# Activation forms moved to other steps, and one split of 1536 columns for the three plain weight units, in a feed-forward loop on one Trainium2 core

## The chip, the cores and the metric

The kernel runs on one core of a Trainium2 chip. The metric is the device time of one execution in microseconds, as the median of several runs. The engines are named as the profile names them: PE is TensorE (PEld its weight loads), DVE VectorE, ACT ScalarE, POOL GpSimd, and SP is SyncE, which here only issues DMAs. Every engine works through its own queue in order and waits at an instruction until what it needs from the others is there.

## The reference

A block of an encoder on 256 tokens of width 2048: two gated branches, an output projection, a layer norm, and a feed-forward part with a second layer norm. Only the feed-forward part matters here:

```python
mix = merged @ w_out[l]
h = _layernorm(DEEPNORM_ALPHA * h + mix, ln1_g[l], ln1_b[l])
ff = jnp.square(jax.nn.relu(h @ w_ff1[l])) @ w_ff2[l]
h = _layernorm(DEEPNORM_ALPHA * h + ff, ln2_g[l], ln2_b[l])
```

w_ff1 is 2048 x 8192 and w_ff2 is 8192 x 2048, both float32.

## The kernel before

Every float32 operand of a matmul is used as a sum of two parts, a high one (hi) and the remainder (lo). ScalarE makes hi by a cast (`cast`, line 1103), VectorE makes lo by a subtraction (`rest`, line 1106). A product is then three matmuls: hi by hi, hi by lo and lo by hi. Weights come from memory as blocks of 1 MB (128 x 2048), and are split on their way.

The hidden width of 8192 is worked on as four quarters of 16 channel blocks. The first product of a quarter (h by w_ff1, `channel_products`, line 141) is made channel block by channel block: eight matmuls of 512 columns and eight of 256 for each half of a block. The second product (by w_ff2) uses, for the first three quarters, a scheme with seven products of sums and differences of activation blocks and weight blocks in place of eight (`FORM`, line 1071, and `join_sums`, line 1262); the last quarter is multiplied directly (`Quarter`, `token_products`).

`ff_pairs` (line 1278) has 48 steps s, and 16 of them are called a phase. In each step it makes one channel block of the next quarter and the seven products of one pair of row blocks of the present one. In the order of the program a step is:

1. three products with the plain weight units (`form_products` which=0, 9 matmuls). Then `plain_split(s + 1)` (line 1156): casts and subtractions of three units of 512 columns, two sums within the raw tile on VectorE, and two DMAs on POOL's queue that add within the raw tile;
2. two products with the first two sums (6 matmuls), and the first half of the channel block;
3. `half_split(s + 1, 0)` and `pair_split(s + 1)`, then two products of the step before (6 matmuls) and `last_split(s)`. These splits are one cast and one subtraction of 1024 columns each;
4. SP's load of the raw tile for step s + 2, and the second half of the channel block;
5. `quad_sum` (line 1109): the channel block's two parts are added out of PSUM, a copy on ScalarE (tile f_l) and a sum on VectorE (tile fr); then `half_split(s + 1, 1)` with SP's load of another block;
6. at some steps `forms` (line 1123), and at odd s `squares` (line 1117), two activations of 512 columns on ScalarE.

Two channel blocks fill one quad tile of 128 x 4 x 128 (`quads`, a ring of five tiles). `forms` turns a finished quad into the seven activation forms of a slot: four casts on ScalarE and six small operations on VectorE, which depend on each other in turn. In the last quarter (`plain`) a form is one cast and one subtraction. There are eight slots (`fa_slot`). Step s reads slot s mod 8, and which=2 reads it once more in step s + 1, so that in a phase of 16 steps slot i is read last in steps 8 + i and 9 + i, and is needed with its new content in step 16 + i. Before, slot i is filled at the end of step 9 + i (line 1305):

```python
if s >= 9 and (s - 9) % 16 < 8:
    forms((s - 9) % 16, s >= 2 * 16 + 9)
```

The last one falls behind the loop and is made in `ff_close` (line 1321).

After each group of eight steps the seven sums are taken out of PSUM (`take_sum`, line 1251), in steps 7, 15, 23 and so on: in the first phase by VectorE (three, with a scale) and ScalarE (four), later by VectorE alone (seven of 512 columns).

The channel products of a step have one PSUM buffer: three of the pool's four are held by sums (w2, w3 and w4), so the next channel block starts when `quad_sum` has read the last one. The tiles of the plain units, `xh` and `wx`, have one buffer each: the cast for step s + 1 waits until the plain products of step s have been made.

Most casts, sums and high-part matmuls of the loop are kept in program order by `pin` (line 1097). What is not pinned, the channel products among it, is ordered by the scheduler when the kernel is built. `ep` is a pool with one buffer for each tag; `turn0` and `turn1` (line 969) are two small tiles of the first layer norm that share a tag and so follow each other. `block_load` (line 1194) puts the blocks of w_ff1 into the tags `xl` and `fraw`.

Of the kernel before, what the change touches and what calls it, by code (L numbers as in the profile page):

```python
# [9 lines left out]
F32 = mybir.dt.float32  # L10
F32R = mybir.dt.float32r
# [5 lines left out]
P = 128  # L17
D = 2048
# [25 lines left out]
def block_kernel(  # L44
# [28 lines left out]
    base = ctx.enter_context(tc.tile_pool(name="base", bufs=1))  # L73
# [175 lines left out]
    with tc.tile_pool(name="xp", bufs=1) as xp, tc.tile_pool(name="xq", bufs=1) as xq:  # L249
        def units(pool, tag, n, **kw):  # L250
            t = pool.tile([P, n, OPENING * P], F32R, tag=tag, name=f"open_{tag}", **kw)
            return lambda a, b: t[:, a:b].rearrange("p k (b j) -> p k b j", b=OPENING)

        pieces = {}
        for k0, n in PIECES[::-1]:
            if k0 < 10:
                pieces[k0] = xp.tile([P, n, KROW], F32, tag=f"xw{k0}", name=f"xw{k0}")
            else:
                raw = wp.tile([P, D], F32, tag="raw", bufs=3, name=f"xw{k0}")
# [15 lines left out]
        for i in range(3):  # L275
            t = weight_half(-1, i)
# [17 lines left out]
        for k0, n in PIECES:  # L294
            raw = pieces[k0]
# [12 lines left out]
            if k0 == 0:  # L308
                hi, lo = places[0]
# [165 lines left out]
    for i in range(2 * NCH):  # L475
        c, o = divmod(i, 2)
        n = 4 + (i * 21) // 15
# [421 lines left out]
    ep = ctx.enter_context(tc.tile_pool(name="ep", bufs=1))  # L899
# [66 lines left out]
    rows1 = load_rows(0)  # L966
    turn_b, turn_i = dfth, dftl
    for i, t in ((0, turn_b), (1, turn_i)):
        raw = ep.tile([P, 1024], F32, tag="wx", name=f"turn{i}")[:, 0:512].rearrange("p (a b) -> p a b", b=P)
        nc.scalar.dma_start(raw, ln_turn[i])  # L970
        nc.scalar.copy(t, raw)
        if i == 0:
            nc.vector.tensor_tensor(t[32:64], raw[32:64], t[32:64].bitcast(F32), op=ALU.subtract)
# [11 lines left out]
    x0 = tuple(ep.tile([P, D], F32R, tag=t, name=t) for t in ("xh", "xl"))  # L985
# [43 lines left out]

    def begin_three():  # L1030
        blocks = [queue.popleft(), [], []]
        hx, lx = (ep.tile([P, D], F32R, tag=t, name=f"{t}_f") for t in ("xh", "xl"))
        at = 0
        for b in (1, 2):
            n = fetched[0]
            fetched[0] = n + 1
            raw = wp.tile([P, D], F32, tag="raw", bufs=3, name=f"raw{n}")
            nc.sync.dma_start(raw, wblk[n])
            for h in range(2):
                src = raw[:, h * 1024:(h + 1) * 1024]  # L1040
                if b + h == 2:
                    hi, lo = hx[:, at:at + 1024], lx[:, at:at + 1024]
                    at += 1024
                    with tc.issue_after(scaled[0].ins):
                        nc.scalar.copy(hi, src)
                    with tc.issue_after(turned[1][1].ins):
                        nc.vector.tensor_tensor(lo, src, hi.bitcast(F32), op=ALU.subtract)
                elif b == 1:
                    hi, lo = weight_half(n, h)
                    split_hi_lo(hi, lo, src)  # L1050
                else:
                    hi, lo = n, src
                blocks[b].append((hi, lo))
        begun = [(channel_psum(f"f0_{b // 2}_{b % 2}"), parts, 1 if b == 2 else 2) for b, parts in enumerate(blocks)]
        for at, size in CHUNKS:
            for ps, parts, n in begun:
# [32 lines left out]
    quad_tiles = [base.tile([P, 4, P], F32, tag=t, name=f"fr{i}") for i, t in enumerate(("dfth", "dftl", "sum"))]  # L1089
    quad_tiles += [ep.tile([P, 4, P], F32, tag=f"fr{i}", name=f"fr{i}") for i in (3, 4)]  # L1090

    def quads(i):
        return quad_tiles[i % 5]

    pinned = [False]

# [6 lines left out]
    def cast(hi, src):  # L1103
        return pin(nc.scalar.copy(hi, src))  # L1104
# [12 lines left out]
    def squares(i):  # L1117
        q = quads(i)
        pin(nc.scalar.activation(q, q, AF.Relu))
        return pin(nc.scalar.activation(q, q, AF.Square))  # L1120


    def forms(i, plain=False):
        q, slot = quads(i), fa_slot(i)
        hi, lo = slot[:, 0], slot[:, 1]
        if plain:
            cast(hi[:, 0:4], q)
            rest(lo[:, 0:4], q, hi[:, 0:4])
            return
        t = base.tile([P, 2, P], F32, tag="as", name=f"fw{i}")  # L1130
        cast(hi[:, 0:3], q[:, 1:4])
        VT(t, q[:, 0:1].broadcast_to([P, 2, P]), q[:, 1:3][:, ::-1], ALU.subtract)
        cast(hi[:, 3:5], t)
        VT(q[:, 0], q[:, 1], t[:, 0], ALU.subtract)
        rest(lo[:, 0:3], q[:, 1:4], hi[:, 0:3])
        VT(q[:, 2], q[:, 3], q[:, 0], ALU.subtract)
        cast(hi[:, 5:7], q[:, 0:3:2])
        rest(lo[:, 3:5], t, hi[:, 3:5])
        rest(lo[:, 5:7], q[:, 0:3:2], hi[:, 5:7])
# [4 lines left out]
            return fa_slot(kt // 2)[:, part, ((1, 0), (3, 2))[kt % 2][ts.start // P]]  # L1144

    SLOTS = 48

    def ring_load(p):
        nc.sync.dma_start(ring_tile(p), wblk[FF_PAIRS + 2 * p])
# [5 lines left out]

    def plain_split(p):
        raw, n = ring_tile(p), FF_PAIRS + 2 * p
        hi = ep.tile([P, D], F32R, tag="xh", name=f"b_h{p}")
        lo = ep.tile([P, 1024], F32R, tag="wx", name=f"b_l{p}")
        u = units(raw)  # L1160
        at = slice(0, 1024), slice(1024, 1536)
        low = lo, hi[:, 1536:2048]
        for c in at:
            cast(hi[:, c], raw[:, c])
        for c, dst in zip(at, low):
            rest(dst, raw[:, c], hi[:, c])
# [111 lines left out]
    def ff_pairs():  # L1278
        pss = [psum_side(f"w{j}") if j not in (2, 3, 4) else psum_main(f"w{j}") for j in range(7)]
        joins = []  # L1280
        for s in range(SLOTS):
            more = s + 1 < SLOTS
            pinned[0] = True
            form_products(pss, s, 0, (0, 1, 2))
            if more:
                plain_split(s + 1)
            form_products(pss, s, 1, (3, 4))
            ps = channel_psum(f"f{s // 16 + 1}_{s % 16}")
            channel_products(ps, hT, half_parts.pop((s, 0)), range(8))
# [11 lines left out]
            i, c = divmod(s % 16, 2)  # L1301
            quad_sum(i, c, ps, f"f{s // 16 + 1}_l{s % 16}")
            if more:
                half_split(s + 1, 1)
            if s >= 9 and (s - 9) % 16 < 8:
                forms((s - 9) % 16, s >= 2 * 16 + 9)
            if c:
                squares(i)
            if joins:
                joins.pop(0)()  # L1310
            pinned[0] = False
            if s == SLOTS - 2:
                stop_at[0] = nblk - 4
                fetched[0] = FF_PAIRS + 2 * SLOTS
            for _ in range(max(0, s - SLOTS + 3)):
                fetch()
        return pss, joins

    def ff_close(pss, joins):
        form_products(pss, SLOTS - 1, 2, (5, 6))  # L1320
        forms(7, True)
        for j in joins + join_sums(1):
            j()

# [25 lines left out]
    def quarters(*tiles):  # L1350
# [4 lines left out]
    own = [ep.tile([P, n], F32R, tag=t, name=f"{t}_r")  # L1355
           for t, n in (("xh", D), ("xl", D), ("fraw", D))]
# [201 lines left out]
```

## Time and profile before

| | before |
|---|---|
| runs, us | 1818.03, 1818.08, 1817.70; median 1818.03 |
| the profiled execution, us | 1818.21, with a span of 1816.4 |
| busy in the span, us | PE 1797.7, PEld 1505.1, DVE 1454.9, ACT 1042.5, POOL 164.8 |
| mean granted clock of TensorE | 0.999 |
| ff_pairs | first weight load of step 0 at 1199.11 us, of step 47 at 1706.84 us |

The page gives busy time by engine. The waits give who waited for whom, with the total, the count and the longest. The table by stage gives busy time in chosen stretches, and the timeline the instructions in order of time: start, duration, engine, line, operation, output and inputs, and in brackets the idle time ahead of it and who ended it. Where instructions of one kind follow each other they are merged, with their count at the end. Matmul records overlap: one of 512 columns shows 0.39 us, and the next begins 0.23 us after it.

### The profile page before, as it was taken

The numbers are of one execution on the slowest core, as the hardware profiler recorded it, in microseconds if no ns is written. First come the engines' busy times: TensorE is split into PE (matmuls) and PEld (weight loads), VectorE is DVE, ScalarE is ACT, GpSimd is POOL, SyncE is SP. The second block draws the span as 40 slices with busy tenths as digits, with TensorE's granted clock in tenths as the row PEclk, the third lists the DMA queues.
The fourth block names the chain that finished last, engine by engine and source line by source line (L and its number), as shares of the span: only waits on it lengthen the run. The fifth ranks groups of instructions, "written<-read, shape, count | busy, mean of one in ns | idle before, by whom it ended". The sixth has DMA issues, their size and how long they took to land.

```text
span 1816.4 us, 23481 instructions
## 1 busy us (share of the span) xinstructions
PE 1797.7 (99%) x8787; PEld 1505.1 (83%) x8787; DVE 1454.9 (80%) x1893; ACT 1042.5 (57%) x1423; POOL 164.8 (9%) x217
## 2 busy tenths in 40 slices
PE   9999999999999999999999999999999999999998
PEld 7888888888888888888888889888877887788887
DVE  6789887875689899988755667688889888989867
ACT  6678668865344444444544445666666566666632
POOL 1011110000111101010000000011111111111100
PEclk9999999999999999999999999999999999999999
DMA  8678876445798979797555764578777977789663
GB/s 324 227 256 292 249 230 200 149 163 204 229 297 250 308 248 283 251 278 258 197 187 186 310 235 159 187 213 248 236 227 235 275 235 221 221 255 273 214 219 127
DMA packets 79283, 424.77 MB, mean 234 GB/s; under 512 B 9817, under 2 KB 12393, under 8 KB 38465
## 3 DMA queue, kind: packets, MB, share of 16 engines
q1 hardware_dynamic: 47808, 336.61, 50.5%
q0 software_dynamic: 24304, 66.99, 18.2%
q10 hardware_dynamic: 7056, 19.67, 3.1%
q8 instruction: 69, 1.13, 0.3%
q14 instruction: 46, 0.37, 0.1%
HBM read 381.86 MB, written 16.25 MB: 219 GB/s over the span
## 4 chain that ended last, share of the span: by engine, by line
PE 87%; DVE 7%; ACT 3%; issue 3%; DMA 1%; ACTq 0%; DVEq 0%; POOL 0%
PE f L147 9%; PE f L151 5%; PE g L200 3%; PE g L199 3%; PE g L201 3%; PE ux L199 3%; PE ux L200 3%; PE ux L201 3%; PE w L1245 3%; PE w L1244 3%; PE w L1246 3%; PE k L147 2%; PE v L201 2%; PE v L200 2%; PE v L199 2%
## 5 line engine op out<-in xcount | busy, mean ns | idle before, releaser
L86 ACT CAST whi<-raw 128x1024 fp32r<-128x1024 f32 x392 | 412.7, 1055 | 408.6 <-PE ux L201 84.4
L87 DVE TENSOR_TENSOR wlo<-raw,whi 128x1024 fp32r<-128x1024 f32 x392 | 477.1, 1221 | 206.8 <-ACT whi L86 205.5
L147 PE MATMUL f<-hT,whi 128*128 128x512 f32 x984 | 246.4, 395 | 2.4 <-DVE fr L1101 1.9
L147 PEld LDWEIGHTS f<-hT,whi 128*128 128x128 f32 x984 | 180.4, 189 | 44.4 <-DVE fr L1101 10.1
L151 PEld LDWEIGHTS f<-hT,wlo 128*128 128x128 f32 x984 | 132.3, 190 | 8.7
L151 PE MATMUL f<-hT,wlo 128*128 128x256 f32 x984 | 135.0, 282 | 0.0
L1101 DVE TENSOR_TENSOR wlo<-fraw,whi 128x1024 fp32r<-128x1024 f32 x96 | 117.0, 1219 | 11.8 <-ACT whi L1104 11.8
L1169 POOL DMA_DIRECT2D ring<-wblk x48 | 41.7, 869 | 723.0 <-DVE ring L1101 723.0
L1104 ACT CAST whi<-ring 128x1024 fp32r<-128x1024 f32 x48 | 50.6, 1054 | 90.6 <-DVE ring L1101 83.8
L1104 ACT CAST whi<-fraw 128x1024 fp32r<-128x1024 f32 x96 | 100.7, 1049 | 0.2 <-PE f L147 0.2
L200 PE MATMUL g<-wlo,xT 128*128 128x512 f32 x256 | 100.1, 391 | 0.0
L201 PE MATMUL ux<-whi,xT 128*128 128x512 f32 x256 | 99.9, 390 | 0.0
L201 PE MATMUL g<-whi,xT 128*128 128x512 f32 x256 | 99.8, 390 | 0.0
L200 PE MATMUL ux<-wlo,xT 128*128 128x512 f32 x256 | 99.6, 389 | 0.0
L199 PE MATMUL g<-whi,xT 128*128 128x512 f32 x256 | 93.8, 392 | 0.0
L199 PE MATMUL ux<-whi,xT 128*128 128x512 f32 x256 | 89.7, 389 | 0.0
L1101 DVE TENSOR_TENSOR b_l<-ring,b_h 128x1024 fp32r<-128x1024 f32 x48 | 58.7, 1224 | 33.1 <-ACT b_h L1104 33.0
L1104 ACT CAST b_h<-ring 128x1024 fp32r<-128x1024 f32 x96 | 74.9, 829 | 8.8 <-ACT whi L1104 8.2
L1101 DVE TENSOR_TENSOR ring<-ring 128x512 f32<-128x512 f32 x96 | 66.0, 688 | 1.6
L1101 DVE TENSOR_TENSOR wlo<-ring,whi 128x1024 fp32r<-128x1024 f32 x48 | 58.8, 1225 | 2.7 <-ACT whi L1104 1.2
L1101 DVE TENSOR_TENSOR fa<-ring,fa 128x1024 fp32r<-128x1024 f32 x48 | 58.5, 1219 | 0.8 <-ACT fa L1104 0.8
L1104 ACT COPY f_l<-f 128x256 f32<-128x256 f32 x64 | 23.7, 370 | 61.1 <-PE f L147 58.2
(538 smaller groups left out, 4345.4 us busy)
## 6 DMA issues: line engine op xcount, KB each, us to landing
raw<-wblk SPq DMA_DIRECT2D x204, 1024.0 KB, 5.1
fraw<-wblk SPq DMA_DIRECT2D x48, 1024.0 KB, 7.1
ring<-wblk SPq DMA_DIRECT2D x48, 1024.0 KB, 6.2
Td<-T POOLq DMA_DIRECT2D x32, 384.0 KB, 5.4
conv_sb<-conv_rows SPq DMA_DIRECT2D x12, 1024.0 KB, 11.5
Tl<-Td POOLq DMA_DIRECT2D x16, 768.0 KB, 9.4
ring<-wblk POOLq DMA_DIRECT2D x48, 256.0 KB, 4.3
ring<-ring POOLq DMA_DIRECT2D x48, 256.0 KB, 5.0
```

Of the source, the lines that this page charges most:

```text
L86: return (nc.scalar.copy(hi, src), nc.vector.tensor_tensor(lo, src, hi.bitcast(F32), op=ALU.subtract))
L87: nc.vector.tensor_tensor(lo, src, hi.bitcast(F32), op=ALU.subtract))
L147: MM(ps[:, :, ts], hi[:, js], act[:, kt, :, ts], start=(kt == 0 and opens), stop=(kt == KT - 1))
L151: MM(ps[:, 0, ts], lo[:, js], act[:, kt, 0, ts], start=False, stop=False)
L199: MM(pss[tb], sh, wh, start=(kt == 0), stop=False)
L200: MM(pss[tb], sh, wl, start=False, stop=False)
L201: MM(pss[tb], sl, wh, start=False, stop=(kt == KT - 1))
L1101: return pin(nc.vector.tensor_tensor(dst, a, b, op=op))
L1104: return pin(nc.scalar.copy(hi, src))
L1244: pin(MM(ps, sh, wh, start=(i == 0), stop=False))
L1245: MM(ps, sh, wl, start=False, stop=False)
L1246: pin(MM(ps, sl, wh, start=False, stop=(i == 7)))
```

## The change

The forms of a phase are made at its steps 9, 11, 13, 15, 17, 18, 20 and 22, counted from the phase's start and running on into the next phase. Forms that fall behind the loop's end (four of the last quarter) are made in `ff_close`. Quads are counted through all quarters (n from 0 to 31), so that the ring of five goes on from one quarter to the next.

The three plain units get one tile of 3072 columns (12 KB a partition, tag `xh`) for hi and lo, in place of `xh` with 2048 and `wx` with 1024, and are split by one cast and one subtraction of 1536 columns, in place of two each of 1024 and 512. The tag `wx` is gone: the turn tiles go to the tag `fraw`. The other tiles under the tag `xh` get the larger size, too, and use its first 2048 columns.

```diff
-        raw = ep.tile([P, 1024], F32, tag="wx", name=f"turn{i}")[:, 0:512].rearrange("p (a b) -> p a b", b=P)
+        raw = ep.tile([P, D], F32, tag="fraw", name=f"turn{i}")[:, 0:512].rearrange("p (a b) -> p a b", b=P)
...
-    def quads(i):
-        return quad_tiles[i % 5]
+    def quads(n):
+        return quad_tiles[n % 5]
...
-    def forms(i, plain=False):
-        q, slot = quads(i), fa_slot(i)
+    def forms(n):
+        q, slot, plain = quads(n), fa_slot(n % 8), n >= 24
...
     SLOTS = 48
+    FORMED = {16 * (q - 1) + s: 8 * q + i for q in range(1, 4) for i, s in enumerate((9, 11, 13, 15, 17, 18, 20, 22))}
...
     def plain_split(p):
         raw, n = ring_tile(p), FF_PAIRS + 2 * p
-        hi = ep.tile([P, D], F32R, tag="xh", name=f"b_h{p}")
-        lo = ep.tile([P, 1024], F32R, tag="wx", name=f"b_l{p}")
+        t = ep.tile([P, 3072], F32R, tag="xh", name=f"b{p}")
+        hi, lo = t[:, 0:1536], t[:, 1536:3072]
         u = units(raw)
-        at = slice(0, 1024), slice(1024, 1536)
-        low = lo, hi[:, 1536:2048]
-        for c in at:
-            cast(hi[:, c], raw[:, c])
-        for c, dst in zip(at, low):
-            rest(dst, raw[:, c], hi[:, c])
+        cast(hi, raw[:, 0:1536])
+        rest(lo, raw[:, 0:1536], hi)
         VT(u[0], u[0], u[3], ALU.add)
         VT(u[3], u[0], u[1], ALU.add)
         nc.gpsimd.dma_start(u[1], wblk[n, :, 1536:2048], accum_op=ALU.add)
         nc.gpsimd.dma_start(u[2], u[3], accum_op=ALU.add)
-        h = units(hi)
-        pieces_of[p, 0] = list(zip(h[:3], units(lo) + h[3:]))
+        pieces_of[p, 0] = list(zip(units(hi), units(lo)))
...
-            if s >= 9 and (s - 9) % 16 < 8:
-                forms((s - 9) % 16, s >= 2 * 16 + 9)
+            if FORMED.get(s, 0) >= 8:
+                forms(FORMED[s])
...
     def ff_close(pss, joins):
         form_products(pss, SLOTS - 1, 2, (5, 6))
-        forms(7, True)
+        for s in range(SLOTS, SLOTS + 8):
+            if s in FORMED:
+                forms(FORMED[s])
```

In the built programs the order on TensorE differs in steps 23 and 39: there the channel products of the step stand behind the first two plain products, ahead of the other plain ones. At the end, two products of the last quarter have changed places with four of the seven-product scheme. On ScalarE and VectorE 48 operations each are gone, the forms have moved, and the copy of the second turn tile stands one cast earlier. On SP's queue the load of one block of w_ff1 (tag `fraw`) stands four loads later. POOL's queue has the same order as before.

More of the change, by code (lines that the diff above doesn't have):

```diff
@@ L984, in block_kernel @@
             add_mix(pss[tb], tb, g * 512, 512)
-    x0 = tuple(ep.tile([P, D], F32R, tag=t, name=t) for t in ("xh", "xl"))
+    x0 = tuple(ep.tile([P, n], F32R, tag=t, name=t)[:, 0:D] for t, n in (("xh", 3072), ("xl", D)))
     parts = resident([x0] + halves(ep, "f", "wr1"))
@@ L1031, in begin_three @@
         blocks = [queue.popleft(), [], []]
-        hx, lx = (ep.tile([P, D], F32R, tag=t, name=f"{t}_f") for t in ("xh", "xl"))
+        hx, lx = (ep.tile([P, n], F32R, tag=t, name=f"{t}_f") for t, n in (("xh", 3072), ("xl", D)))
         at = 0
@@ L1115, in quad_sum, with squares @@
             VT(dst, halves[0], halves[1], ALU.add)
-    def squares(i):
-        q = quads(i)
+    def squares(n):
+        q = quads(n)
         pin(nc.scalar.activation(q, q, AF.Relu))
         return pin(nc.scalar.activation(q, q, AF.Square))
-    def forms(i, plain=False):
-        q, slot = quads(i), fa_slot(i)
+    def forms(n):
+        q, slot, plain = quads(n), fa_slot(n % 8), n >= 24
         hi, lo = slot[:, 0], slot[:, 1]
@@ L1129, in forms @@
             return
-        t = base.tile([P, 2, P], F32, tag="as", name=f"fw{i}")
+        t = base.tile([P, 2, P], F32, tag="as", name=f"fw{n}")
         cast(hi[:, 0:3], q[:, 1:4])
@@ L1300, in ff_pairs @@
             channel_products(ps, hT, half_parts.pop((s, 1)), range(8, 16))
-            i, c = divmod(s % 16, 2)
-            quad_sum(i, c, ps, f"f{s // 16 + 1}_l{s % 16}")
+            n, c = divmod(s + 16, 2)
+            quad_sum(n, c, ps, f"f{s // 16 + 1}_l{s % 16}")
             if more:
                 half_split(s + 1, 1)
-            if s >= 9 and (s - 9) % 16 < 8:
-                forms((s - 9) % 16, s >= 2 * 16 + 9)
+            if FORMED.get(s, 0) >= 8:
+                forms(FORMED[s])
             if c:
-                squares(i)
+                squares(n)
             if joins:
@@ L1354, in block_kernel @@
     spare = [t[:, 7168:8192] for t in fa]
-    own = [ep.tile([P, n], F32R, tag=t, name=f"{t}_r")
-           for t, n in (("xh", D), ("xl", D), ("fraw", D))]
+    own = [ep.tile([P, n], F32R, tag=t, name=f"{t}_r")[:, 0:D] for t, n in (("xh", 3072), ("xl", D), ("fraw", D))]
     parts = resident_pieces(quarters(*own, *spare)
```

## The prediction

> **What bounds the kernel now.** I read the page first, then TensorE's waits, then a table by stage, then single steps of the feed-forward part.
>
> ```profile
> span 1816.4 us, 23481 instructions
> PE 1797.7 (99%) x8787; PEld 1505.1 (83%) x8787; DVE 1454.9 (80%) x1893; ACT 1042.5 (57%) x1423; POOL 164.8 (9%) x217
> ```
> ```profile
> PE w L1245 <- DVE wlo L1101: 6.6, 8, 1.8
> PE w L1244 <- ACT whi L1104: 1.0, 5, 0.2
> ```
> TensorE is busy for 99% of the span. What waits it has lie almost all in the 48 steps of ff_pairs and end on the weight splits (tiles whi and wlo). The table by stage shows where. Columns: stretch, its length, busy us and count of PE, PEld, DVE, ACT, POOL, the granted clock, DMA share, GB/s.
>
> ```profile
> 1311.55:1404.23 92.68, 88.01 (x425) 69.59 (x424) 82.73 (x119) 61.70 (x91) 15.00 (x18) 1.00 0.76 226
> 1404.23:1487.01 82.78, 82.78 (x426) 70.87 (x425) 70.37 (x85) 51.01 (x66) 13.15 (x15) 1.00 0.87 256
> 1487.01:1582.22 95.21, 89.36 (x426) 70.63 (x424) 85.03 (x123) 59.74 (x87) 14.98 (x18) 0.98 0.74 220
> ```
> The stretches are cut at the first weight load of steps 11, 19, 27 and 35, eight steps each. Steps 19 to 26 hold no forms and TensorE never idles: 82.78 / 8 = 10.35 us is a free step. Steps 11 to 18 take 92.68, that is 9.90 too much, and steps 27 to 34 take 95.21, 12.43 too much. These are the steps behind forms at s = 9 to 16 and 25 to 32. In steps 40 and 41 it happens once more, in small:
>
> ```profile
> 1633.95 0.19 PEld L1244 LDWEIGHTS w<-b_h,fa 128*128 128x128 f32 x1
> ...
> 1655.11 0.19 PEld L1244 LDWEIGHTS w<-b_h,fa 128*128 128x128 f32 x1
> ```
> 21.16 - 2 x 10.35 = 0.46. So 9.90 + 12.43 + 0.46 = **22.8 us** is all that this change can win.
>
> How a form costs time is seen in step 10, where the first form of a phase (emitted at the end of s = 9) runs:
>
> ```profile
> 1301.42 0.39 PE L1244 MATMUL w<-b_h,fa 128*128 128x512 f32 x1
> ```
> ```profile
> 1301.68 0.37 ACT L1104 COPY f_l<-f 128x256 f32<-128x256 f32 x1 [1.75 <-PE f L147]
> 1301.95 1.06 ACT L1104 CAST whi<-fraw 128x1024 fp32r<-128x1024 f32 x1
> 1302.90 0.52 ACT L1104 CAST fa<-fr 128x384 fp32r<-128x384 f32 x1
> 1304.63 0.41 ACT L1104 CAST fa<-fw 128x256 fp32r<-128x256 f32 x1 [1.22 <-DVE fw L1101]
> 1305.75 0.41 ACT L1104 CAST fa<-fr 128x256 fp32r<-128x256 f32 x1 [0.72 <-DVE fr L1101]
> ...
> 1306.72 0.63 ACT L1120 ACTIVATE fr<-fr 128x512 f32<-128x512 f32 x1
> 1307.26 1.55 ACT L1104 CAST b_h<-ring 128x1024 fp32r<-128x1024 f32 x2
> ```
> ```profile
> 1308.33 1.23 DVE L1101 TENSOR_TENSOR b_l<-ring,b_h 128x1024 fp32r<-128x1024 f32 x1 [1.71 <-ACT b_h L1104]
> ...
> 1310.07 1.41 DVE L1101 TENSOR_TENSOR ring<-ring 128x512 f32<-128x512 f32 x2
> 1311.40 1.22 DVE L1101 TENSOR_TENSOR wlo<-fraw,whi 128x1024 fp32r<-128x1024 f32 x1
> 1312.66 1.23 DVE L1101 TENSOR_TENSOR wlo<-ring,whi 128x1024 fp32r<-128x1024 f32 x1
> 1313.80 1.22 DVE L1101 TENSOR_TENSOR fa<-ring,fa 128x1024 fp32r<-128x1024 f32 x1
> 1314.93 0.42 DVE L1101 TENSOR_TENSOR fr<-f,f_l 128x256 f32<-128x256 f32 x1
> ```
> ```profile
> 1315.41 2.11 PE L147 MATMUL f<-hT,whi 128*128 128x512 f32 x8
> ```
> ScalarE and VectorE hand the form back and forth, then come the squares (odd steps only, some 1.2 us), and only then the cast of the next plain units. VectorE stands 1.71 us for it, then has no gap up to the sum of the last channel product at 1314.93, whose PSUM tile TensorE needs again. Step 11 begins 10.35 after step 10, and its f starts at 1315.41 in place of 1301.42 + 10.35 + 15 x 0.227 = 1315.18. So one lone form in an odd step uses up the whole lead of the splits (about 3 us) and overruns by 0.2 to 0.4: step 11 is 0.36 long. With a form in every step nothing is won back: an even form step behind an odd one overruns by
>
> ```profile
> 1322.26 0.19 PEld L1244 LDWEIGHTS w<-b_h,fa 128*128 128x128 f32 x1
> ...
> 1333.30 0.19 PEld L1244 LDWEIGHTS w<-b_h,fa 128*128 128x128 f32 x1
> ```
> 11.04 - 10.35 = 0.69, an odd one by more.
>
> **The change part by part.** *One split of 1536.* 48 casts and 48 subtractions fall away.
>
> ```profile
> L780 DVE TENSOR_TENSOR pb<-Z,Tl 128x1536 f32<-128x1536 f32 x16 | 28.0, 1749 | 0.0
> ```
> ```profile
> L301 ACT CAST open_yT<-xw 128x1280 fp32r<-128x1280 f32 x2 | 2.5, 1259 | 0.0
> L1104 ACT CAST b_h<-ring 128x1024 fp32r<-128x1024 f32 x48 | 50.0, 1042 | 8.8 <-ACT whi L1104 8.2 <-ACT zr L1104 0.3 <-ACT fa L1104 0.2
> ```
> On VectorE 1536 columns take 1.75 us. Followed directly by another operation, some 0.09 of that is overlapped, 1.66 against 1310.07 - 1308.33 = 1.74 for the two: 0.08 won. On ScalarE I extend 1280 and 1024 columns in a line: 1.26 + 0.217 = 1.48, against 1.55 for the two. But the subtraction now starts when all 1536 are cast, 1.48 after the cast begins and not 1.04. In a free step the lead covers it, at no cost. Where VectorE stands for that cast, as at 1308.33, the chain is 0.44 - 0.08 = **0.35 longer**. Bounds: -0.08 (no wait there) to 0.51 (the cast as long as the pair). I take 0.35, since the row of this very place shows the wait. The Trainium skill, "VectorE: DVE Perf Modes", section on the TRN2 errata, says that a fixed latency is paid per instruction, so one large tile is better than several small ones. The trace agrees on the busy time (1.75 for 1536 columns, 1.23 for 1024); by that rule alone the chain would be 0.08 shorter, not 0.35 longer, which would take some 4 us off the sum.
>
> *Forms at 9, 11, 13, 15, 17, 18, 20, 22.* VectorE is busy for 70.37 / 8 = 8.8 us of a free step, so it has 1.5 us to spare, and the 1.71 us behind the squares does not come again in the step after an odd form: the lead is back before the next form. So 9, 11 and 13 are lone odd forms: 0.36 + 0.35 = 0.7 each, 2.1 in a phase. The form at 17 is another, 0.7; the one at 18 follows it, 0.69 + 0.35 = 1.0; the one at 20 is lone and even, with no squares, 0. The form at 15 meets the sums of a finished group of eight:
>
> ```profile
> 1545.57 1.28 DVE L1101 TENSOR_TENSOR zr<-zr,w 128x512 f32<-128x512 f32 x2
> ```
> 0.6 us each, three on VectorE in the first phase, seven in the second. Bounds 0.7 (hidden) to 0.7 + 1.8 = 2.5 and to 0.7 + 4.2 = 4.9. I take 1.5 and 3.3, above the middle in the second, where ScalarE takes none of them.
>
> *The last form, at 22.* It fills the slot that step 23 reads first of all. Before it was emitted at 16 and had six steps. ScalarE's queue in the changed program reads: f_l of step 22, whi half, form cast of 384. By the rows of step 10 that cast ends at 1302.90 + 0.52 - 1301.42 = 2.0 us after the step's end, so TensorE stands 2.05 us. In the built program the scheduler puts the channel products of step 23 ahead of most of its plain products, so the rest of the form (ready by about 5 us) is covered. But the plain products then end late. A matmul of 512 columns is issued every 0.227 us (15 of them in the 3.41 us above), one of 256 every 0.12:
>
> ```profile
> 1553.95 1.12 PE L151 MATMUL f<-hT,wlo 128*128 128x256 f32 x8
> ```
> The third plain product stands behind 28 of the one and 16 of the other and a slower first matmul: 2.05 + 0.1 + 6.36 + 1.92 = 10.4 us, in a free step 2.0. The cast of the next plain units waits for it (they use one tile): 10.7 to 12.1. VectorE's queue follows, without a gap: subtraction 12.1, ring sums 13.8, two sums of this group of eight (take_sum) 15.1, wlo half 16.3, wlo pair 17.5 to 18.7, last unit 18.6, sum of f 19.7 to 20.15. TensorE's f of step 24 starts at 20.2, in a free run at 10.35 + 3.41 = 13.75. So this form costs **6.5 us** (2.05 in step 23, the rest in step 24), and the same at steps 39 and 40. Bounds: 2.05 (the lead covers all that follows) to 8. I take 6.5: every row of the chain is in the trace.
>
> *Third phase.* Forms at 41, 43, 45, 47 and four behind the last step, without pins; two operations of 0.6 each, beside token products that need them 11 us later: 0.
>
> *turn under fraw.* Its tile moves, and with it the load of the second block of ff1 weights goes four loads later on SP's queue, still some 100 us ahead of its use; ScalarE's copy of the second turn moves up by one cast. 0; if that DMA is late, up to 3. POOL's two accumulating DMAs of a step keep their order and come 0.35 later in form steps; their data are used a step later.
>
> Sum: first phase 2.1 + 1.5 + 0.7 + 1.0 + 6.5 = 11.8, second 2.1 + 3.3 + 0.7 + 1.0 + 6.5 = 13.6; together 25.4, in place of 22.8: **+2.6 us**.
>
> *The clock.* One row of before belongs to the price:
>
> ```profile
> 1546.85 0.19 PEld L1244 LDWEIGHTS w<-whi,fa 128*128 128x128 f32 x1 [0.62 <-ACT whi L1104]
> 1549.17 0.19 PEld L1245 LDWEIGHTS w<-wlo,fa 128*128 128x128 f32 x1 [2.14 <-DVE wlo L1101]
> ```
> ```profile
> 1551.00:1552.00 1.00, 1.00 (x3) 0.80 (x3) 1.00 (x2) 0.00 (x0) 0.00 (x0) 0.50 0.72 127
> ```
> ```profile
> 1550.66 3.45 PE L147 MATMUL f<-hT,whi 128*128 128x512 f32 x8
> ...
> 1557.25 2.00 PE L147 MATMUL f<-hT,whi 128*128 128x512 f32 x8
> ```
> Two waits, 2.76 us in all with one matmul between, and the granted clock falls to 0.50 for about 3 us: eight matmuls take 3.45 in place of 2.1, 1.35 us lost. In step 24 I expect much the same pair, 0.5 for the cast of the pair and 2.0 for its wlo, and again in step 40. Bounds 0 to 4 falls (steps 23, 24, 39, 40); I take one, 1.35. The total is 2.6 + 1.35 = **+4.0 us**: 1818.21 + 4.0 = 1822.2 for a run like the profiled one, which is 0.18 above the median of the runs, so 1822.0.
>
> **The rivals.** *The clock holds* (chance 0.25). The waits of step 24 are apart, and in before no other step fell. Then 1818.03 + 2.6 = 1820.7. This is also what the Trainium skill makes of it, "TensorE: Matmul & The Clock Gate", Part 1: the gate judges a free-running window of about 3.4 us, so waits shorter than that should not re-throttle. The trace speaks against it, since 0.62 and 2.14 were enough.
>
> *The late form is hidden* (0.08): ScalarE or the order of TensorE keeps steps 23, 24, 39 and 40 free. Then 13 us go out of the sum: 1818.0 - 10.4 = 1807.6, faster. For it: a form in the middle of a phase costs little. Against it: ScalarE runs in order, and f_l, which is ahead of the form, waits for TensorE's end of step 22.
>
> *Worse stalls* (0.17): the cast of 1536 takes 1.6, the lead is not won back in one step, and the clock falls at each of four places: 2.6 + 4 x 1.35 + 8 x 0.1 = 8.8, 1826.8.
>
> *The change does nothing that can be measured*: the lone forms cost 0.36 as before, since the wide split's delay is covered: 22.6 against 22.8, with or without a fall of the clock 1818 to 1819.3 (0.12).
>
> **How the numbers follow.** The forecast, stalls with one or two falls of the clock, has 0.38; its own range is 1820.5 to 1824. The predicted time is 1822.0. The clock at rest and the does-nothing case pull the range down to 1819, the worse case up to 1826. A change of 0.2%, 3.6 us, is about what a measurement of this kernel can tell from none. The forecast lies 0.4 above that mark, so 0.27 of its 0.38 is slower, with 0.17 of the worse case and 0.10 of the clock's: slower 0.54. Same: the remainder of the forecast and of the clock's (0.11 and 0.15) and 0.11 of the does-nothing case: 0.37. Faster 0.09.
>
> **What would show it.** Right: steps 11, 13, 15 some 0.7 us long, 12, 14 and 16 free; a wait of 2 us on ScalarE's form cast at the first plain product of steps 23 and 39; steps 24 and 40 over 4 us long with waits on wlo; steps 25 and 41 free. The VectorE row of 128x1536 at 1.75, ScalarE's near 1.48. Wrong: no wait at step 23, or a wait in steps 24 and 40 of under 1 us, or lone forms that cost nothing.

## The result, and the profile after

| | before | after |
|---|---|---|
| median, us | 1818.05 (1817.70 to 1819.01, 4 runs) | 1831.53 (1830.25 to 1831.94, 4 runs) |
| profiled execution: span, us | 1816.4 | 1830.1 |

The ratio is 1.0072, 95% interval 1.0059 to 1.0085: slower by 13.5 us. The prediction said slower, but by 4.0, and its range ended at 1826.0.

The first lines of the page of after, and the two groups of the wide split (count, total busy us, mean ns):

```profile
span 1830.1 us, 23299 instructions
...
PE 1801.6 (98%) x8787; PEld 1506.6 (82%) x8787; DVE 1455.8 (80%) x1845; ACT 1037.0 (57%) x1375; POOL 164.6 (9%) x217
```
```profile
L1102 DVE TENSOR_TENSOR b<-ring,b 128x1536 fp32r<-128x1536 f32 x48 | 84.3, 1757 | 49.1 <-ACT b L1105 48.8
...
L1105 ACT CAST b<-ring 128x1536 fp32r<-128x1536 f32 x48 | 70.6, 1471 | 19.3 <-PE w L1243 14.2
```
The durations are as forecast, 1.757 and 1.471 us. What the forecast left out is in the last column: VectorE stands 48.8 us in all for this one cast. In before it stands 33.0 us for the two casts in its place (total, count, longest):

```profile
DVE b_l L1101 <- ACT b_h L1104: 33.0, 34, 1.7
```
TensorE's waits in after:

```profile
PE w L1242 <- DVE wlo L1102: 7.9, 14, 1.8
PE w L1241 <- ACT fa L1105: 4.8, 2, 2.4
PE f L147 <- DVE fr L1102: 2.8, 4, 1.2
PE w L1242 <- DVE b L1102: 2.3, 2, 1.1
```
Two kinds are new against before: the waits of steps 23 and 39 on ScalarE's form cast (fa), and waits of the plain products on their own low parts (b). The table by stage, cut at steps 11, 22 and 26, and at 27, 38 and 41:

```profile
1310.86:1431.17 120.31, 117.36 (x584) 96.50 (x583) 104.26 (x128) 76.45 (x98) 19.35 (x22) 1.00 0.80 240
1431.17:1482.86 51.69, 45.40 (x214) 35.99 (x212) 41.70 (x49) 28.10 (x33) 8.76 (x10) 0.97 0.69 203
1493.21:1615.80 122.59, 118.45 (x585) 96.25 (x583) 106.57 (x132) 74.52 (x94) 19.34 (x22) 1.00 0.78 236
1615.80:1658.43 42.63, 36.10 (x160) 28.32 (x159) 34.81 (x43) 22.44 (x27) 7.01 (x8) 0.92 0.64 187
```
A free step is 10.35. Steps 11 to 21 are 120.31 - 11 x 10.35 = 6.5 long, steps 22 to 25 10.3, steps 27 to 37 8.7, and steps 38 to 40 11.6: **37.1 us of stalls** in place of 22.8. The loop starts 0.7 earlier; 14.3 - 0.7 is the 13.7 us between the spans to 0.1. So the two stretches around the late form hold 22 of the 37 us. Its weight loads with waits, in the first phase:

```profile
1433.85 0.19 PEld L1242 LDWEIGHTS w<-wlo,fa 128*128 128x128 f32 x1 [0.45 <-DVE wlo L1102]
1435.32 1.69 PEld L147 LDWEIGHTS f<-hT,whi 128*128 128x128 f32 x8 [0.46 <-DVE fr L1102]
1444.96 0.19 PEld L1241 LDWEIGHTS w<-b,fa 128*128 128x128 f32 x1 [2.82 <-ACT fa L1105]
1458.59 0.19 PEld L1242 LDWEIGHTS w<-b,fa 128*128 128x128 f32 x1 [1.56 <-DVE b L1102]
1461.20 0.19 PEld L1241 LDWEIGHTS w<-whi,fa 128*128 128x128 f32 x1 [0.92 <-ACT whi L1105]
1463.51 0.19 PEld L1242 LDWEIGHTS w<-wlo,fa 128*128 128x128 f32 x1 [2.12 <-DVE wlo L1102]
1464.98 1.01 PEld L147 LDWEIGHTS f<-hT,whi 128*128 128x128 f32 x5 [0.48 <-DVE fr L1102]
```
Step 22 already stands twice before its own form is reached; then step 23 stands for the late form, and step 24 at every split in turn.

### The profile page after: what moved, and what is told of

Read it like the earlier page. It is cut to its first block, busy times and chain, and to the rows that moved or that the text cites. A ratio compares the mean times of both kernels' runs of the same rounds, so it can differ in the third digit from the quotient of the medians.

```text
span 1830.1 us, 23299 instructions
## 1 busy us (share of the span) xinstructions
PE 1801.6 (98%) x8787; PEld 1506.6 (82%) x8787; DVE 1455.8 (80%) x1845; ACT 1037.0 (57%) x1375; POOL 164.6 (9%) x217
## 4 chain that ended last, share of the span: by engine, by line
PE 85%; DVE 8%; ACT 4%; issue 2%; DMA 0%; ACTq 0%; SPq 0%; DVEq 0%
PE f L147 9%; PE f L151 4%; PE g L200 3%; PE g L199 3%; PE g L201 3%; PE ux L199 3%; PE ux L200 3%; PE ux L201 3%; PE w L1242 2%; PE w L1241 2%; PE w L1243 2%; DVE b L1102 2%; PE r L199 2%; PE r L201 2%; PE r L200 2%
## 5 line engine op out<-in xcount | busy, mean ns | idle before, releaser
L1102 DVE TENSOR_TENSOR b<-ring,b 128x1536 fp32r<-128x1536 f32 x48 | 84.3, 1757 | 49.1 <-ACT b L1105 48.8
L1105 ACT CAST b<-ring 128x1536 fp32r<-128x1536 f32 x48 | 70.6, 1471 | 19.3 <-PE w L1243 14.2
L1241 PE MATMUL w<-b,fa 128*128 128x512 f32 x144 | 56.8, 394 | 4.8 <-ACT fa L1105 4.8
L1242 PE MATMUL w<-b,fa 128*128 128x512 f32 x144 | 56.9, 395 | 2.3 <-DVE b L1102 2.3
```

The costliest lines, as they stand in the source:

```text
L1102: return pin(nc.vector.tensor_tensor(dst, a, b, op=op))
L1241: pin(MM(ps, sh, wh, start=(i == 0), stop=False))
L1242: MM(ps, sh, wl, start=False, stop=False)
```

## The experiments

"Stalls" is the time from step 11 to step 47 in its trace, less 36 free steps (372.5 us). The medians come out at 1795 + stalls within 0.8 us, so nearly all of each difference lies in these steps. The median of before is that beside the experiments.

| kernel | forms at | plain split | stalls | median, us |
|---|---|---|---|---|
| before | 9 to 16 | 1024 + 512 | 22.8 | 1817.8 |
| e5 | 9 to 16 | 1024 + 512, one tile | 22.8 | 1817.69 |
| e1 | as the change | 1024 + 512, one tile | 22.4 | 1817.94 |
| e2 | 9 to 16 | 1536 | 30.6 | 1825.24 |
| after | as the change | 1536 | 37.1 | 1831.53 |
| e4 | as the change | cast 1536, subtraction in two | 32.2 | 1827.41 |
| e3 | the change, last at 21 | 1536 | 25.0 | 1819.83 |
| e9 | 9, 11, 13, 15, 16, 17, 18, 22 | 1536 | 34.5 | 1829.64 |
| e6 | 9, 10, 12, 14, 16, 18, 20, 21 | 1024 + 512 | 10.2 | 1805.84 |
| e7 | as e6, behind the plain split | 1024 + 512 | 10.9 | 1805.73 |
| e8 | 9 to 16, behind the plain split | 1024 + 512 | 22.4 | 1817.46 |
| e10 | as e6 | 1536 | 22.9 | 1817.91 |
| e13 | as e6 | 3 x 512 | 5.6 | 1800.58 |
| e14 | as e6, squares behind | 1024 + 512 | 3.5 | 1799.04 |
| e15 | as the change, squares behind | 1536 | 18.1 | 1813.79 |
| e16 | as e6, squares behind | 3 x 512 | 2.5 | 1797.50 |

### One part of the change at a time (e1, e2, e5)

e1 keeps the forms and the tile and splits in two pieces; e2 keeps the wide split and puts the forms back; e5 has only the tile.

```diff
-        cast(hi, raw[:, 0:1536])
-        rest(lo, raw[:, 0:1536], hi)
+        at = slice(0, 1024), slice(1024, 1536)
+        for c in at:
+            cast(hi[:, c], raw[:, c])
+        for c in at:
+            rest(lo[:, c], raw[:, c], hi[:, c])
```
```diff
-    FORMED = {... enumerate((9, 11, 13, 15, 17, 18, 20, 22))}
+    FORMED = {... enumerate((9, 10, 11, 12, 13, 14, 15, 16))}
```


> Forms at 9 to 22 as in the change, the plain units split in two pieces as before (1024 and 512), in the new tile. Theory (the late form and the clock fall it brings are most of the cost, the wide split adds 0.48 us wherever VectorE stands for its cast): lone odd forms back at 0.36 us, no wait left in step 22, the wait at the first plain product of step 23 about 2.1 us and no longer 2.6, steps 22 to 25 some 8 us too long in place of 10.3; 1819 to 1823 us. Rival (the wide split is what makes the change slow, the late form only shows it): 1812 us or less, with steps 23 and 24 under 2 us too long.

> Wide split as in the change, forms back at steps 9 to 16. Theory: every form step pays 0.48 us more than before, eight in each phase, so 1818 + 16 x 0.48 = 1825.7 us, and steps 23, 24, 39 and 40 are free. Rival (the wide split is hidden but for the late form): 1818 us.

> Of the change only the tile of 3072 columns and the moved turn tile are left: forms at 9 to 16, casts and subtractions in two pieces. Theory (the tile costs nothing by itself; all of the change's time is in the two other parts): stalls as in before, 22.8 us, and the loop begins some 0.7 us earlier as in the other kernels with this tile, so 1817.0 to 1818.3, same as before. Rival (the large tile or the later load of a block costs something that the other runs hid): 1820 or more.

e1: 1817.94, ratio 1.0002 (0.9992 to 1.0011). e2: 1825.24, 1.0041 (1.0026 to 1.0055). e5: 1817.69, 0.9999 (0.9990 to 1.0009). So the tile costs nothing, the moved forms by themselves come out at nothing, and the wide split by itself costs 7.8 us of stalls, as the theory said. But 7.8 and -0.4 don't add up to 14.3: the two parts make each other worse by 7 us. e1 was better than its theory. Its lone odd forms cost 0.37 (0.85 in after). The late form costs it 4.5 in steps 22 to 25, and 8.3 in steps 38 to 40, where its trace has two falls of the clock; these 12.8 us eat up what the spread forms save in the other steps. Its waits in the first of the two places:

```profile
1441.00 0.19 PEld L1244 LDWEIGHTS w<-b,fa 128*128 128x128 f32 x1 [2.24 <-ACT fa L1105]
1455.50 0.19 PEld L1245 LDWEIGHTS w<-wlo,fa 128*128 128x128 f32 x1 [1.97 <-DVE wlo L1102]
1456.97 1.69 PEld L147 LDWEIGHTS f<-hT,whi 128*128 128x128 f32 x8 [0.48 <-DVE fr L1102]
```
Step 22 has no wait, the wait for the form cast is 2.24 in place of 2.82, and two of the waits of step 24 are gone. Part of that is order: in e1 as it was built, five channel products of 512 columns and seven of 256 fewer stand ahead of the last plain products of step 23.

### The late form, and which half of the split (e3, e4)

```diff
-    FORMED = {... enumerate((9, 11, 13, 15, 17, 18, 20, 22))}
+    FORMED = {... enumerate((9, 11, 13, 15, 17, 18, 20, 21))}
```
```diff
+        at = slice(0, 1024), slice(1024, 1536)
         cast(hi, raw[:, 0:1536])
-        rest(lo, raw[:, 0:1536], hi)
+        for c in at:
+            rest(lo[:, c], raw[:, c], hi[:, c])
```


> The change with the last form of a phase at step 21 in place of 22. Theory: the wait of step 23 on the form's cast, the order of TensorE that it brings, the clock falls and the stalls of step 24 all go; one more odd form behind an even one costs about 2 us a phase: 1831.5 - 21.9 + 4 to 6 = 1814 to 1816 us. Rival (a step earlier only moves the stall, since two forms stand side by side): 1825 us or more.

> The change with the cast of 1536 kept and the subtraction in two pieces of 1024 and 512. Theory (0.44 of the 0.48 is the longer wait for the cast, 0.05 is the sum within the raw tile, which must wait until the wide subtraction has read that tile): lone odd forms 0.80 us in place of 0.85, 1830 us. Rival (the wide subtraction is what costs): lone odd forms 0.4 us and 1824 us or less.

e3: 1819.83, 1.0012 (1.0002 to 1.0021): 11.7 below after, one step earlier for one form. Steps 22 to 25 fall from 10.3 to 4.3, steps 38 to 41 from 11.6 to 5.3, and the granted clock stays at 1.00. It missed its theory by 4: the pair of forms at 20 and 21 costs these 4.3 and 5.3 us, where some 2 a phase were reckoned. e4: 1827.41, 1.0053 (1.0038 to 1.0068), between the two expectations. Its lone odd steps are 0.80 long against 0.85, so nearly all of the wide split's delay is the wide cast. Of the 4.9 us by which its stalls are below those of after, 4.0 lie in steps 38 to 41, where its order on TensorE and its falls of the clock (one in place of two) differ too; that part was not separated.

### Three steps of rest ahead of the late form (e9)

```diff
-    FORMED = {... enumerate((9, 11, 13, 15, 17, 18, 20, 22))}
+    FORMED = {... enumerate((9, 11, 13, 15, 16, 17, 18, 22))}
```


> The change, with the forms of 18 and 20 moved up to 16 and 18 and so at 9, 11, 13, 15, 16, 17, 18 and 22: three steps without a form ahead of the last one. The verdict lies in the trace of steps 22 to 25 and 38 to 41; four forms in a row make steps 17 to 20 and 33 to 36 some 2.5 us dearer in each phase. Theory (in the change the lead was not won back when the last form came: step 22 was 0.6 late and the wait at step 23 was 2.8 in place of 2.05): steps 21 and 22 are free, the wait at step 23 is 2.0 to 2.3, and steps 22 to 25 cost 8 to 9 with one fall of the clock, 6.5 to 7.5 without, against 10.3. In all 1829 to 1836. Rival (the late form costs what it costs whatever comes before): a wait of 2.8 again, and over 10 us with a fall.

1829.64, 1.0064 (1.0049 to 1.0079). Steps 21 and 22 are free, and the low parts of step 22 are ready 4.6 us ahead of its first product, against 1.2 in after. The wait at step 23 didn't come as expected: in this build TensorE makes a half channel block of step 23 ahead of its plain products, and waits 1.34 for fr. Steps 22 to 25 cost 6.3 without a fall. The changed kernel, in an execution without a fall there (e12, below), has in steps 22 to 25 and 38 to 41:

```profile
1431.45:1481.53 50.08, 43.76 (x214) 34.88 (x213) 41.67 (x49) 28.10 (x33) 8.78 (x10) 1.00 0.69 209
1615.91:1666.64 50.73, 43.76 (x214) 34.89 (x213) 44.37 (x55) 27.13 (x33) 7.44 (x9) 1.00 0.69 208
```
50.08 - 4 x 10.35 = 8.7, and in the second phase (steps 38 to 41) 9.3. So with the lead intact the late form costs about what was predicted (6.5), and some 2.4 us more without. How much of the 2.4 is the lead and how much the order on TensorE stays open.

### Where a form stands (e6, e7, e8)

e6 splits in two pieces as e1 and puts most forms in even steps, where no squares follow. e7 and e8 move each form behind the next step's plain split, with the steps of e6 and of before.

```diff
             if more:
                 plain_split(s + 1)
+            if FORMED.get(s - 1, 0) >= 8:
+                forms(FORMED[s - 1])
             form_products(pss, s, 1, (3, 4))
...
-            if FORMED.get(s, 0) >= 8:
-                forms(FORMED[s])
```


> Two pieces as in before, forms at 9, 10, 12, 14, 16, 18, 20 and 21: all but two in even steps, where no squares follow them, and none at 22. Theory (a lone form costs only where the squares follow it ahead of the next plain cast): the steps behind 12, 14, 16, 18 and 20 are free, 9 costs 0.4, 10 behind it 0.7, 21 behind 20 about 1 and 0.3 more with the sums of the group of eight; some 2.5 to 3.5 in a phase, no fall of the clock: 1799 to 1805. Rival (spreading only moves the stalls about, as in the kernel with spread forms and two pieces, which came out at 1817.94): 1812 or more.

> As the kernel with forms at 9, 10, 12, 14, 16, 18, 20 and 21 in two pieces, but each form stands behind the next step's split of the plain units in the queues of ScalarE and VectorE, in place of ahead of it. Theory (what costs time is that VectorE stands 1.7 us for a plain cast that waits behind form and squares on ScalarE): the waits go in all steps, 1795 to 1799. Rival (the form's own 1.5 us on VectorE and the to and fro between the engines set the stall, wherever they stand): no more than 1.5 us from the kernel it is made from.

> Two pieces and the forms of before (9 to 16), but each form behind the next step's split of the plain units. Against before only the place in the two queues differs. Theory (the wait of VectorE behind form and squares is most of a form's price): of the 22.8 us at least half goes: 1798 to 1808. VectorE then has some 10.35 us of work in each of eight steps in a row, so a part stays, most of all where the sums of a group of eight come too. Rival (VectorE's load in eight steps in a row is what costs, not the order): 1815 or more.

e6: 1805.84, 0.9935 (0.9918 to 0.9952), 12 us faster than before. It is 0.8 above the expected interval: the sums of a group of eight at steps 32 and 40 and the pair 20, 21 cost more than estimated. e7: 1805.73, and e8: 1817.46 against 1817.8. Here the rivals were right: the place of the form against the plain cast is worth nothing. In e8 VectorE's waits for the plain cast (between 1199 and 1700 us) shrink from 32.1 us to 26.3, and those for the casts whi grow from 11.9 to 20.3.

### The wide split with few stalls (e10)

e6 with the two lines of the wide split.

> The forms of the fast kernel (9, 10, 12, 14, 16, 18, 20 and 21) with the wide split of the change. Theory (a wide split delays its readers by some 0.5 us wherever a stall stands, and costs nothing in a free step): the fast kernel has some 14 long steps, so 5 to 8 us more than its 1805.8: 1811 to 1814. Rival (the dear part of the wide split was its meeting with the late form at 22, and with few stalls it costs nothing): 1805 to 1808.

1817.91, 0.9999 (0.9990 to 1.0009): 12 us more than e6. Both expectations missed; the split costs more where there are *fewer* stalls. Step 13 of e6 and of e10 behind the same lone form, ScalarE's cast, then VectorE:

```profile
1338.23 1.56 ACT L1105 CAST b<-ring 128x1024 fp32r<-128x1024 f32 x2
```
```profile
1339.30 1.83 DVE L1102 TENSOR_TENSOR b<-ring,b 128x1024 fp32r<-128x1024 f32 x2 [0.52 <-ACT b L1105]
1341.04 1.41 DVE L1102 TENSOR_TENSOR ring<-ring 128x512 f32<-128x512 f32 x2
```
```profile
1339.30 1.47 ACT L1105 CAST b<-ring 128x1536 fp32r<-128x1536 f32 x1
```
```profile
1340.80 1.76 DVE L1102 TENSOR_TENSOR b<-ring,b 128x1536 fp32r<-128x1536 f32 x1 [0.95 <-ACT b L1105]
1342.59 1.42 DVE L1102 TENSOR_TENSOR ring<-ring 128x512 f32<-128x512 f32 x2
```
From the start of the cast to the ring sum it is 1341.04 - 1338.23 = 2.81 and 1342.59 - 1339.30 = 3.29: 0.48 longer. VectorE has no gap of over 0.2 us in this step but the one for the cast, so the 0.48 of each plain split stays in its queue. The subtraction shown ends at 1341.13 in e6 and at 1342.56 in e10, which is 2.1 and 1.25 us ahead of the first product of step 14 (1343.22 and 1343.81). From step 14 on every second step of e10 is 0.64 long or more, while e6 is free up to step 17. VectorE's waits for the plain cast between 1199 and 1700 us (total, count, longest), in e6 and in e10:

```profile
DVE b L1102 <- ACT b L1105: 32.9, 36, 1.7
```
```profile
DVE b L1102 <- ACT b L1105: 47.9, 38, 2.1
```
15.0 us more standing on VectorE becomes 12.7 us of stalls on TensorE. A fall of the clock in step 32 of e10, where e6 has none, is in the 12.7.

### The other way: finer pieces, and squares out of the way (e13 to e16)

e13 is e6 with three casts and three subtractions of 512, the opposite of the change. e14 is e6 with the squares behind the next plain split; e15 the changed kernel with that alone; e16 has both.

```diff
-        at = slice(0, 1024), slice(1024, 1536)
+        at = slice(0, 512), slice(512, 1024), slice(1024, 1536)
```
```diff
             if more:
                 plain_split(s + 1)
+            if s and s % 2 == 0:
+                squares((s + 15) // 2)
...
-            if c:
+            if c and not more:
                 squares(n)
```


> The fast kernel (forms at 9, 10, 12, 14, 16, 18, 20 and 21), with the three plain units split by three casts and three subtractions of 512 columns in place of 1024 and 512: the opposite of the change. Theory (VectorE has next to no slack in steps with forms, and what it stands for the first finished cast goes straight into the step): the first subtraction starts some 0.5 us earlier, the last ends some 0.3 earlier after 0.1 more of work, and about half of the fast kernel's 10.2 us of stalls goes: 1800 to 1803. Rival (each operation more costs its fixed part on both engines): 1806 or more.

> The fast kernel, with the squares of an odd step behind the next step's split of the plain units on ScalarE, in place of ahead of it. Theory (VectorE stands for the plain cast mostly because the squares run first, 1.2 us of its 1.7): its wait for that cast falls from 32.9 us in the loop to under 12, and most of the 10.2 us of stalls goes: 1796 to 1801. Rival (as with the forms moved behind the split, the wait only turns up at another cast): 1804 to 1808.

> The changed kernel, with the squares behind the next step's plain split and nothing else. Theory: the lone odd forms (11, 13, 15, 19 and their like, 0.85 us each) become free, and step 22 is not late any more; the last form at 22 stays, at 7 to 8.5 us a phase with up to two falls of the clock: 1815 to 1823. Rival: 1828 or more.

> The fast kernel with both: three pieces of 512 and the squares behind the split. Theory: next to no stall is left, 1795 to 1799, the better of the two single edits or below. Rival: no better than the fast kernel's 1805.8.

e13: 1800.58, 0.9904 (0.9889 to 0.9918). e14: 1799.04, 0.9895 (0.9880 to 0.9910). e15: 1813.79, 0.9977 (0.9967 to 0.9986), 17.7 below after by this edit alone. e16: 1797.50, 0.9886 (0.9870 to 0.9903), the fastest: 20 us below before. All four went the way of their theory; e15 came out 1.2 below its interval. In e15 steps 22 to 25, around the late form, are 5.6 long without a fall. The row of VectorE's waits for the plain cast, in e13 and in e14, where it is 12.4 and was expected under 12:

```profile
DVE b L1102 <- ACT b L1105: 16.6, 24, 1.3
```
```profile
DVE b L1102 <- ACT b L1105: 12.4, 24, 0.5
```
The stalls follow it: 22.9 at 47.9 us, 10.2 at 32.9, 5.6 at 16.6, 3.5 at 12.4. Unlike the moved forms of e7 and e8, the moved squares pay: what reads them, a form, comes steps later. Part of the wait turns up elsewhere here, too (from e6 to e14, for the casts whi 8.2 to 12.5 us, for f_l 7.8 to 15.4), but the stalls fall all the same. In e16 the row is gone, and VectorE waits for the products:

```profile
DVE fr L1102 <- ACT f_l L1105: 18.2, 22, 1.8
```
The rival's fixed price of an operation is there, too: VectorE is busy 1457.8 us in e13 against 1453.8 in e6, and e13 is 5 us faster.

## Why the prediction was wrong

The direction, most places and the durations were right, the size was not. Stalls of the first phase (steps 11 to 25), predicted and measured, without the clock in the first column:

| step | predicted | measured in after |
|---|---|---|
| 11, 13, 15 | 0.7 each | 0.83, 0.85, 0.85 |
| 12, 14, 16, 18, 21 | 0 | 0 |
| 17 | 1.5 | 1.92 |
| 19 | 0.7 | 0.85 |
| 20 | 1.0 | 1.17 |
| 22 | 0 | 0.6 |
| 23 and 24 | 6.5 | 9.0, a fall of the clock in it |
| 25 | 0 | 0.66 |

- **The chain of the wide split**, 0.35, is 0.48. The wide subtraction does take 1.757, but the ring sum starts 1.79 after it and not 1.66: the 0.09 of overlap isn't there. The likely reason, not tested, is that the first sum writes a part of the raw tile that the subtraction still reads.

```profile
1428.18 1.76 DVE L1102 TENSOR_TENSOR b<-ring,b 128x1536 fp32r<-128x1536 f32 x1 [0.95 <-ACT b L1105]
1429.97 1.42 DVE L1102 TENSOR_TENSOR ring<-ring 128x512 f32<-128x512 f32 x2
```
- **"The lead is back before the next form"** is the step that failed, for the forms at 20 and 22. The lead is the time by which VectorE's low parts are ready ahead of the products that read them. Behind the lone odd forms it was back: the subtraction for step 12 ends at 1316.19 + 1.75 = 1317.94, 4.1 us ahead of that step's first product (1322.04), and steps 12, 14 and 16 are free. The one for step 22, shown above, ends at 1429.94, only 1.2 ahead (1431.17), and step 22 is 0.6 long, where the form at 20 was reckoned at 0. An odd form and its squares stand ahead of the same plain cast, and VectorE waits once, 2.13 us. With an even form they stand ahead of two casts in a row, and it waits 0.95 (above) and 1.59:

```profile
1308.07 1.76 DVE L1102 TENSOR_TENSOR b<-ring,b 128x1536 fp32r<-128x1536 f32 x1 [2.13 <-ACT b L1105]
1316.19 1.75 DVE L1102 TENSOR_TENSOR b<-ring,b 128x1536 fp32r<-128x1536 f32 x1
...
1437.99 1.76 DVE L1102 TENSOR_TENSOR b<-ring,b 128x1536 fp32r<-128x1536 f32 x1 [1.59 <-ACT b L1105]
```
The 1.5 us to spare were reckoned from VectorE's busy time, 8.8 of 10.35 us, without such waits; with one of 1.59 nothing is left. The wide split makes them longer (1.17 at the same place of e1, whose step 22 has no wait). So after the forms at 17, 18 and 20 the program comes to the late form with its lead short, and step 23 waits 2.82 in place of 2.05.

- **The late form at 22**, 6.5, is 8.7 and 9.3 in the two phases without a fall (e12); this is the term most off. The mechanism was as described, a wait at step 23 on ScalarE's cast, the plain products behind the channel products, and the splits of step 24 behind them; e3 shows that the form's place alone is worth 12 us, falls of the clock included. The forecast had it begin with the full lead, and took step 25 as free (0.66); with the full lead e9 has 6.3, in another order on TensorE. The forecast also left out the wait of 1.56 for the plain products' low parts (b) in step 24: the wide subtraction hands over all low parts at its end, so the products get the first of them 1.471 - 1.04 = 0.43 (the cast) and 1.757 - 1.23 = 0.53 later than from a piece of 1024.
- **One fall of the clock for 1.35 us** was three, and they cost 3.9 us: steps 22 to 25 and 38 to 41 are 10.3 and 11.6 long in after, 8.7 and 9.3 in e12 without a fall. A fall takes up to 1.7 us, half of 3.41, but some of it comes back (step 41, 0.68 long in e12, is free in after). In after they follow the wait of 2.8 at steps 23 and 39 and the pair of 2.13 and 1.07 in step 40; none follows step 24, where one was expected.

Of the 10.4 us by which the stalls exceed the forecast (37.1 against 25.4 + 1.35), 3.9 - 1.35 = 2.5 is the clock, 15.2 - 12.4 = 2.8 the steps of the forms up to 18, and 18.0 - 13 = 5.0 the steps around the late form in the two phases, to 0.1.

Of the rivals, "worse stalls" was the nearest. The causes that it named, a longer cast and a lead not won back, were half right: the cast is no longer than forecast, and the lead is not won back behind the even form at 20. "The clock holds" fell with the three falls. The rows bear out the Trainium skill, "VectorE: DVE Perf Modes", section on the TRN2 errata, by which a large operation pays a fixed latency once and small ones each time, for the operation by itself: the wide subtraction takes 1.757 us, the two in its place 1.83. VectorE's busy time as a whole is not less for it, 1454.9 us in e10 against 1453.8 in e6. And no time is gained: e13, with more operations, is 17 us faster than e10.

## What to carry to other kernels

When one engine casts and another subtracts, the size of a piece sets how long the second stands for the first; where that second engine has no slack, as here, fusing two pieces lengthens the wait in every iteration, and cutting finer won. Look for an operation that no one waits for soon (here the squares) ahead of one that an engine stands for, and swap them before moving anything larger. And sum an engine's work over the steps *with* the extra work and with its waits: a lead that is "won back in the next step" has to be found in the idle time of those steps.

## What the runs showed of the hardware

In these runs the clock is judged on a fixed grid. In the loop every fall to 0.50 but one lasts 3.41 us, and the falls of one execution lie whole multiples of 3.413 us apart. Table by stage with the stretches cut on that grid, first of after, then of a second and a third execution of the same kernel (e11, e12). The third figure from the right is the granted clock; rows stand in pairs, a window and the one behind it.

```profile
1441.69:1445.10 3.41, 1.01 (x5) 0.51 (x4) 3.37 (x5) 3.22 (x5) 1.75 (x2) 1.00 0.74 176
1445.10:1448.51 3.41, 3.41 (x9) 2.63 (x10) 3.20 (x7) 0.81 (x2) 0.00 (x0) 0.50 1.01 290
1462.17:1465.58 3.41, 2.02 (x8) 1.36 (x9) 3.41 (x5) 1.76 (x3) 0.11 (x1) 1.00 0.92 151
1465.58:1468.99 3.41, 3.41 (x20) 2.97 (x19) 1.81 (x2) 2.96 (x4) 0.00 (x0) 1.00 0.88 327
```
```profile
1462.19:1465.60 3.41, 1.74 (x6) 1.16 (x7) 3.41 (x5) 1.76 (x4) 0.40 (x1) 1.00 0.88 149
1465.60:1469.01 3.41, 3.41 (x10) 2.70 (x9) 1.82 (x2) 3.24 (x4) 0.00 (x0) 0.50 0.98 315
```
```profile
1441.04:1444.45 3.41, 1.78 (x8) 1.12 (x6) 3.37 (x4) 2.89 (x4) 1.76 (x2) 1.00 0.80 282
1444.45:1447.86 3.41, 2.63 (x12) 2.22 (x13) 3.34 (x8) 1.14 (x3) 0.00 (x0) 1.00 0.96 203
```


> The changed kernel once more, for a second profiled execution. Theory (the clock is judged in windows of some 3.41 us on a fixed grid that runs freely, and falls to half for the next window when TensorE stood 2.1 us or more in one): the waits are the same to 0.1 us, but which of them are followed by a fall depends on where they lie on this execution's grid; all falls of the execution begin a whole number of 3.413 us apart, each behind a window with 2.1 us or more of standing, and no window with under 1.9 is followed by one. Rival (the fall belongs to the wait itself): falls at steps 23, 39 and 40 again and none at step 24. 1829.5 to 1832.5 by either.

> The changed kernel a third time, with the same two readings: by the grid the falls lie elsewhere or not by the grid's place against the waits, by the rival at steps 23, 39 and 40. 1829.5 to 1832.5.

The waits that no fall lies ahead of were the same to 0.03 us, and the falls were elsewhere: at steps 23, 24 and 40 in e11 (1831.66), at step 33 alone in e12 (1829.97). So the rival, a fall that belongs to a wait, is out. What decides is TensorE's busy time (first figure behind the length) within a window: with 1.74 us of 3.41 or less the next window runs at half clock, with 1.78 or more it doesn't. Over all eighteen executions, between 1300 and 1665 us, this holds for 19 windows below and 28 of 1.78 to 2.2. (By the waits of the weight loads, as the expectation has it, it is 2.10 us of standing in the window of e11 and 2.05 in that of e12.) Each grid was laid by a fall of its own execution. Five have two or three falls in the loop, and there the multiples test it (20.48 = 6 x 3.413 in e11). In those with one, the fall behind TensorE's last product does: in e12 it begins 262.83 = 77 x 3.413 us behind the one in step 33. One window that was already slow, in e4, was followed by another at half clock with 2.29 us busy.

So the limit is about half a window, and a wait of 2.1 us costs up to 1.7 more or nothing, by where it falls. The Trainium skill, "TensorE: Matmul & The Clock Gate", Part 1, gives a free-running window of 3413 ns: the traces agree on its length and that it runs freely. They don't agree that it takes an idle window; 1.7 us of idling inside one was enough. The prediction had one fall to go by, from which neither the threshold nor the place of the grid could be read.
